# First stage of a decoder trunk: rows of x, norms and rotary tables requested earlier, sums of x halves placed in the weights' order, ordinary units regrouped around products

## The chip, the cores and the metric

The kernel runs on one core of a Trainium2 chip. The metric is device time in microseconds (us) of one execution. Each engine runs its own instructions in the order in which they were issued to it: TensorE (PE in the profile) multiplies, VectorE (DVE) and ScalarE (ACT) work element by element, GpSimd (POOL) does small element-wise work and issues some DMAs, and SyncE (SP) issues most DMAs.

## The reference

A trunk of two layers over x, 256 rows of 2048, in float32. Layer 0 uses differential attention with rotation of the first quarter of each head, layer 1 latent attention; each layer then attends to 256 memory rows and applies a squared-ReLU MLP. Every sub-layer is pre-normed and added to x. The change touches only the beginning of layer 0:

```
h = rms_norm(x, attn_norm[0])
q, k, v = split(h @ da_wqkv, 3)              # 2048 -> 3 x 2048
q = partial_rope(q, cos, sin, 32); k = partial_rope(k, cos, sin, 32)
p = softmax(mask(q k^T / sqrt(128)))         # two maps per head, 8 heads
a = p[map 0] - lam * p[map 1]                # lam from lam_vecs
x = x + rms_norm(a v, subln) * 0.8 @ da_wo
```

The gain of the norm goes into the transposed x ahead of the product; the factor of each row (rstd) is applied behind it, when a product leaves PSUM.

## The kernel before

**A float32 product in three passes.** Each operand is split into a high part in the type that TensorE multiplies fast and a low part, the rest. A product is three matmuls: high x high, high x low, low x high. Activations are split once, weights as they come: a tile of weights (128 x 2048, 1 MB) is loaded by `load` (line 165, SP's queue) into one of seven raw buffers, ACT casts each half of it to `whi` (line 195) and DVE subtracts to get `wlo` (line 196). Four buffers each of `whi` and `wlo` hold two tiles, so ACT and DVE can be two tiles ahead of PE.

**Units and products.** An ordinary unit is one weight tile against both halves of the rows (t = 0, 1): 24 matmuls of 128 x 128 x 512. Where a whole 2048 x 512 projection of both halves of the rows and of two column blocks is wanted, `Seven` and `Chained` compute a 2 x 2 block product with seven products, p1 to p7, instead of eight (in the order p1, p5, p3, p7, p2, p6, p4). A product is two weight tiles of 12 matmuls each, so it uses up weight tiles twice as fast as ordinary units do. Some products take sums of weight blocks: for p5 DVE adds two raw tiles (line 874, `Chained.begin`), for p7, p6 and p4 a POOL DMA adds a block of weights onto a raw tile that an earlier product has used (line 798). The matching sums of x blocks, s1 to s4, are formed once by `GivenForms`: line 459 first adds the high and low part of a given unit of x back together, lines 429, 396 and 397 then form and split the sums.

**Order.** PE's order is written out: the program emits matmuls in sequence, and small tasks (`Task`, a generator that yields delays) are stepped by `pump` when a running count of PE time, `clock`, has passed their due time. So a transpose stands in PE's stream at a place given by its delay, whether or not its input is ready then. The other engines' instructions are ordered by a planner from a simulated timeline, with two exceptions: DMAs keep the program's order on their queue, and instructions marked `in_turn` (the `wlo` subtractions and raw sums) keep the program's order among themselves.

**The first stage.** Four units of x transposed (`xT`) come in with the gains applied (`given_unit`, line 324). Then PE does q of head group 0 (four ordinary units), k of group 0 (four), and three lines, one for each next head group: line gi holds the seven products for q and k of group gi + 1, with eight ordinary units between. In line 0 these are the v of group 0 and the v of group 1; in the other lines, the output projection of the group before and the next v. `diff_line` writes down where the ordinary units stand. Attention of group gi runs as tasks inside line gi.

`take` hands out a split weight tile, refills the list of tiles that are being split, and calls a hook by the number of tiles taken. The hooks bring in what the first units do not need: hook 1 loads the constants (identity, mask, frequencies), hooks 2 to 6 the rows of x in eight pieces of 128 x 512 with a sum of squares by ACT each (line 330), hook 6 also the positions and the vectors for lambda, then rstd (lines 342, 335, 336, 1074), the rotary tables and lambda, and hook 7 starts `GivenForms`.

Behind q and k, `heads_T` evacuates PSUM with the row's factor (line 487, ACT), rotates (lines 498 to 503, six POOL operations), and, after a delay, transposes four heads on PE (line 159) and splits them (lines 296 and 297). With `given` it first waits until the factors have been issued. Its transposes go into the same PSUM bank, or with `spare=True` into a bank from a small side pool.

Of the kernel before, what the change touches and what calls it, by code (L numbers as in the profile page):

```python
# [14 lines left out]
ALU = mybir.AluOpType  # L15
AX = mybir.AxisListType

P = 128
# [11 lines left out]
T_EV, T_TURN, T_ROT, T_SM, T_SQ, T_ADD, T_NORM = 2.6, 2.6, 12.0, 6.5, 4.4, 2.2, 6.5  # L30
# [11 lines left out]
C_ID, C_MASK, C_FREQ, NC_ = 0, 128, 256, 256 + NF  # L42
# [3 lines left out]
def trunk(ctx, tc, x, xT, mem, memT, positions, gcols, gfinal, lam_vecs, consts, W, out):  # L46
    nc = tc.nc
# [19 lines left out]
    def unit():  # L67
        return units.tile([P, 2, 4, S], F32R, tag="unit", name=nm("unit"))
# [78 lines left out]
    def give_back():  # L147
        free_banks[0] += 1
# [12 lines left out]
    def f32(ap):  # L161
        return ap.bitcast(F32)

    def load(dst, src, queue=None):
        tc.keep_in_program_order((queue or nc.sync).dma_start(dst, src))


    def in_turn(ins):
        tc.stamp_issue_order_token(ins.ins, "weights")
        return ins  # L170
# [39 lines left out]
    def fill():  # L210
        while len(ready) < AHEAD and plan:
            job = plan.pop(0)
            if callable(job) and job not in begun:
                job.begin()
            if plan and callable(plan[0]):
                begun.append(plan[0])
                plan[0].begin()
            if callable(job):
                ready.append(job())
            else:  # L220
                name, i, width = job
                ready.append(split_weights(W[name][i, :, : 4 * width], width))

    taken = [0]
    hooks = {}

    def take():
        fill()
        got = ready.pop(0)
        fill()  # L230
        taken[0] += 1
        if taken[0] in hooks:
            hooks[taken[0]]()
        return got

    def unit_part(o, a, h, hi, lo, t, first, last):
# [43 lines left out]
    const = work.tile([P, NC_], F32, tag="ev", name="const", padded_shape=[P, CH], bufs=EVS)  # L280
    g = keep.tile([P, NG], F32, name="g")
    pos = keep.tile([P, NT], I32, name="pos")
    lamv = work.tile([P, 4, P], F32, tag="ev", name="lamv", bufs=EVS)
    xs = [keep.tile([P, D], F32, name=f"x{t}") for t in range(NT)]
    identr = keep.tile([P, P], F32R, name="identr")
    ident = f32(identr)
    maskr = keep.tile([P, P], F32R, name="maskr")
# [88 lines left out]
    class Forms(Stream):  # L376
# [37 lines left out]
        def sums(self):  # L414
            for key in [(t, h) for t in range(NT) for h in range(2)]:
                for task in self.forms[key].tasks:
                    yield task
            for x in range(2):
                views = [self.raw[t][:, 8 * h + 4 * x : 8 * h + 4 * x + 4] for t in range(NT) for h in range(2)]
                for _ in self.sums_of(x, *views):  # L420
                    pass
                yield T_TURN
# [21 lines left out]
    class GivenForms(Forms):  # L444
# [9 lines left out]
        def sums(self):  # L454
            for x in range(2):
                rows = f32(unit()).rearrange("p a k t -> p (a k) t")
                for h in range(2):
                    part = self.units[2 * h + x].tile
                    nc.vector.tensor_tensor(rows[:, 4 * h : 4 * h + 4], f32(part[:, 0]), f32(part[:, 1]), ALU.add)
                    yield T_TURN  # L460
                views = [rows[:, 4 * h : 4 * h + 4, t * P : (t + 1) * P] for t in range(NT) for h in range(2)]
                for _ in self.sums_of(x, *views):
                    yield T_TURN
# [38 lines left out]
        e.tensor_tensor(a, m[0], m[1], ALU.subtract)  # L502
        e.tensor_tensor(b, n[0], n[1], ALU.add)

    def heads_T(ps, t, scale, dst, rot=None, spare=False, given=None):


        def task():
            while given and not given():
                yield 0.5  # L510
            e = evacuate(ps, scale() if given else scale)
            if rot:
                cos, sin, heads, half = rot
                rope(e.rearrange("p (h d) -> p h d", h=heads), cos, sin, heads, half)
            yield T_ROT + (10.0 if given else 0.0) if rot else T_EV
            b = ps
            if spare:
                b = yield from side_bank()
            split(dst, t, transpose4(e, b))
            if spare:  # L520
                give_back()
            yield T_TURN

        dst.run(task())
# [408 lines left out]
    def diff_line(gi):  # L933
        values_of = lambda g: [("da_wqkv", 12 * g + 8 + u, CH) for u in range(4)]
        others = values_of(0) if gi == 0 else [("da_wo", 4 * c + gi - 1, CH) for c in range(4)]
        others = [Item(None, None, [job]) for job in others + values_of(gi + 1)]
        seven = Chained("da_wqkv", 3 * (gi + 1)).items()
        lead = 0 if gi else 3
        line = others[:lead]
        del others[:lead]  # L940
        for n in (1, 1, 1, 1, 1, 2, 1) if gi else (0, 1, 0, 1, 1, 2, 0):
            line += seven[:2] + others[:n]
            del seven[:2], others[:n]
        return line
# [43 lines left out]
    acts = []  # L988
# [21 lines left out]
    def x_pieces(at, n):  # L1010
        for t, c in [(t, c) for t in range(NT) for c in range(4)][at : at + n]:
            xc = xs[t][:, c * CH : (c + 1) * CH]
            load(xc, x[t * P : (t + 1) * P, c * CH : (c + 1) * CH])
            sum_squares(norm.ss[t][:, c : c + 1], xc)

    def first_norm():
        x_pieces(6, 2)
        load(pos, positions)
        load(lamv, lam_vecs)
        norm.rstd = [row_norm(norm.ss[t], D)[:, 0:1] for t in range(NT)]  # L1020
        da_scales.append(keep2(norm.rstd, SC_DA, "rq"))
        da_scales.append(keep2(norm.rstd, 1.0, "r1"))
        tables()

    def tables():

        nc.vector.tensor_copy(posf, pos)
        for t in range(NT):
            nc.vector.tensor_scalar(ang[:, t], const[:, C_FREQ : C_FREQ + NF], posf[:, t : t + 1], None, ALU.mult)
        MAGIC = 1.5 * 2.0**23  # L1030
        PI_LE = 3.1415925
        nc.vector.tensor_scalar(turn, ang, 1.0 / (2.0 * math.pi), MAGIC, ALU.mult, ALU.add)
        nc.vector.tensor_scalar(turn, turn, MAGIC, None, ALU.subtract)
        for part in (6.28125, 0.0019350051879882812, 2.0 * math.pi - 6.28125 - 0.0019350051879882812):
            nc.vector.scalar_tensor_tensor(ang, turn, -part, ang, ALU.mult, ALU.add)
        nc.vector.tensor_scalar(ang, ang, PI_LE, -PI_LE, ALU.min, ALU.max)
        nc.scalar.activation(sin, ang, AF.Sin)
        nc.vector.tensor_scalar(turn, ang, math.pi / 2.0, -2.0 * math.pi, ALU.is_gt, ALU.mult)
        nc.vector.scalar_tensor_tensor(ang, ang, math.pi / 2.0, turn, ALU.add, ALU.add)
        nc.vector.tensor_scalar(ang, ang, PI_LE, -PI_LE, ALU.min, ALU.max)  # L1040
        nc.scalar.activation(cos, ang, AF.Sin)


        lv = lamv.rearrange("p (a b) d -> p a b d", b=2)
        nc.vector.tensor_tensor(lp, lv[:, :, 0, :], lv[:, :, 1, :], ALU.mult)
        nc.vector.tensor_reduce(ls, lp, AX.X, ALU.add)
        nc.scalar.activation(ls, ls, AF.Exp)
        nc.vector.memset(coef, 1.0)
        nc.vector.tensor_tensor(coef[:, 1:2], ls[:, 1:2], ls[:, 0:1], ALU.subtract)
        nc.vector.tensor_scalar(coef[:, 1:2], coef[:, 1:2], -LAMBDA_INIT, None, ALU.add)  # L1050
        nc.vector.tensor_copy(coef[:, 3:4], coef[:, 1:2])
        for i in range(2):
            nc.vector.tensor_scalar(gsub[:, 2 * i : 2 * i + 2], g[:, G_SUB : G_SUB + 2], 1.0 - LAMBDA_INIT, None, ALU.mult)
        nc.scalar.copy(identr, const[:, C_ID : C_ID + P])
        nc.scalar.copy(maskr, const[:, C_MASK : C_MASK + P])
    mem_rstd = []

    def mem_norm():
# [168 lines left out]


    da_scales = []
    hooks[1] = lambda: load(const, consts)  # L1230
    hooks[2] = lambda: x_pieces(0, 1)
    hooks[3] = lambda: x_pieces(1, 1)
    hooks[4] = lambda: x_pieces(2, 2)
    hooks[5] = lambda: x_pieces(4, 2)
    hooks[6] = first_norm
    hooks[7] = lambda: made.append(GivenForms(acts))
    made = []

    hd = DA_ROT // 2

    def rotation(t):
        return cos[:, t, :hd], sin[:, t, :hd], 4, hd
# [53 lines left out]
    for i, dst in enumerate((q, k)):  # L1296
        ps = matmul_chunk(acts)
        for t in range(NT):
            heads_T(ps[t], t, lambda i=i, t=t: da_scales[i][t], dst, rotation(t), given=lambda: da_scales)
    v, before, copied = [], None, {}  # L1300
    free_banks[0] -= 1
    for gi, line in enumerate(diff_lines):
# [32 lines left out]
    acts = norm.done()  # L1335
# [31 lines left out]
    ps = matmul_chunk(acts, LAT)  # L1367
    latent_piece(eq, 0, ps, 0, LAT)
    ps = matmul_chunk(acts, LAT)
# [4 lines left out]
    ps = matmul_chunk(acts, 320)  # L1374
# [186 lines left out]
```

## Time and profile before

| what | value |
|---|---|
| median of 3 runs | 2236.24 us (2235.97 to 2236.39) |
| profiled execution | 2237.54 us |
| its span, first to last instruction | 2235.4 us |
| mean granted TensorE clock | 0.996 |
| HBM read | 499 MB, 224 GB/s over the span |

The profile's page lists busy times by engine and the costliest groups of instructions. The view of windows gives busy times in chosen stretches; the timeline lists instructions in order, and its brackets hold the idle time ahead of an instruction on its engine and what ended it; the chain of waits follows the work that ended last back to the start. In all of them L155 is the matmul helper, L159 the transpose helper, `mm` an ordinary product, `pr` one of the seven, `ax` side work.

### The profile page before, as it was taken

Reading aid. Unit: us, or ns where it says so; the run is one execution under the profiler, and the core shown is the slowest. Engines: PE = TensorE matmul, PEld = TensorE weight load, DVE = VectorE, ACT = ScalarE, POOL = GpSimd, SP = SyncE. Lnnn points to the kernel's source line nnn. Section 1 sums busy time; section 2 is a strip of 40 time slices with the busy share of each in tenths; the row PEclk is TensorE's granted clock in tenths of the full one; section 3 lists DMA queues with packets and bytes.
Section 4 is the critical chain, followed back from the end, with each engine's and each line's share of the span. In section 5 each row is a group of like instructions: output and inputs, shape, how many; then the busy total and the mean of one; then the engine's idle time right before and its main releaser. Section 6 shows DMA issues by size and latency. Waiting matters only on the chain.

```text
span 2235.4 us, 27536 instructions
## 1 busy us (share of the span) xinstructions
PE 2213.1 (99%) x10449; PEld 1842.8 (82%) x10449; DVE 1742.5 (78%) x1921; ACT 1415.4 (63%) x1905; POOL 186.8 (8%) x268
## 2 busy tenths in 40 slices
PE   9999999999999999999999999999999999999998
PEld 7778888888888888888889888888888888888886
DVE  8777877778888888888765766778887887887864
ACT  7666667666666666666645655566666666666664
POOL 0241120000000000000000311000000000000001
PEclk9999999999999999999999999999999999999999
DMA  9679887435886887886945244634688688688691
GB/s 381 177 245 254 268 256 260 162 126 195 270 272 214 264 269 218 263 271 216 294 163 193 87 155 146 256 131 153 231 248 272 234 244 272 235 243 272 228 304 57
DMA packets 75445, 502.96 MB, mean 225 GB/s; under 512 B 8625, under 2 KB 9009, under 8 KB 17201
## 3 DMA queue, kind: packets, MB, share of 16 engines
q1 hardware_dynamic: 64080, 422.56, 50.9%
q0 software_dynamic: 10656, 77.60, 17.8%
q8 instruction: 82, 1.34, 0.2%
q10 hardware_dynamic: 576, 1.05, 0.2%
q14 instruction: 51, 0.41, 0.0%
HBM read 499.08 MB, written 2.10 MB: 224 GB/s over the span
## 4 chain that ended last, share of the span: by engine, by line
PE 91%; DVE 4%; ACT 1%; issue 1%; DMA 1%; POOL 0%; ACTq 0%; POOLq 0%; DVEq 0%
PE mm L155 61%; PE pr L155 24%; PE ax L155 3%; PE ax L159 2%; DVE wlo L196 2%; DVE raw L795 2%; DMA raw<-in_da_wqkv_dram 1%; ACT whi L195 1%; PE mm L159 1%; DVE unit L297 0%; DVE unit L531 0%; DVE raw L874 0%; DVE unit L324 0%; POOL rope L500 0%; DVE unit L711 0%
## 5 line engine op out<-in xcount | busy, mean ns | idle before, releaser
L196 DVE TENSOR_TENSOR wlo<-raw,whi 128x1024 fp32r<-128x1024 f32 (+3 forms) x998 | 1197.2, 1212 | 406.0 <-ACT whi L195 373.8
L195 ACT CAST whi<-raw 128x1024 fp32r<-128x1024 f32 (+3 forms) x998 | 1038.0, 1042 | 687.8 <-PE mm L155 487.2
L155 PE MATMUL mm<-whi,unit 128*128 128x512 f32 (+3 forms) x4160 | 1326.5, 390 | 1.4 <-ACT unit L615 0.9
L155 PEld LDWEIGHTS mm<-whi,unit 128*128 128x128 f32 x4160 | 779.6, 189 | 153.8 <-ACT unit L323 1.3
L155 PE MATMUL mm<-wlo,unit 128*128 128x512 f32 (+3 forms) x2080 | 805.4, 387 | 6.8 <-DVE wlo L196 6.3
L155 PE MATMUL pr<-whi,unit 128*128 128x512 f32 x1904 | 612.9, 391 | 0.0
L155 PEld LDWEIGHTS mm<-wlo,unit 128*128 128x128 f32 x2080 | 392.5, 189 | 86.9 <-DVE wlo L196 15.2
L155 PEld LDWEIGHTS pr<-whi,unit 128*128 128x128 f32 x1904 | 357.4, 188 | 73.8
L155 PE MATMUL pr<-wlo,unit 128*128 128x512 f32 x952 | 370.7, 389 | 0.0
L155 PEld LDWEIGHTS pr<-wlo,unit 128*128 128x128 f32 x952 | 178.9, 188 | 36.3
L798 POOL DMA_DIRECT2D raw<-in_mlp_wup_dram x56 | 49.1, 877 | 1119.0 <-DVE wlo L196 985.2
L795 DVE TENSOR_TENSOR raw<-raw,raw 128x2048 f32<-128x2048 f32 x56 | 127.9, 2284 | 0.0
L482 DVE TENSOR_TENSOR x<-x,mm 128x512 f32<-128x512 f32 x152 | 99.8, 680 | 11.3 <-PE mm L155 10.7
L336 POOL TENSOR_TENSOR rs<-rs,mhalf 128x1 f32<-128x1 f32 (+1 forms) x28 | 26.2, 939 | 556.8 <-DVE rs L335 556.8
L296 ACT CAST unit<-ax 128x512 fp32r<-128x512 f32 (+1 forms) x100 | 55.8, 571 | 25.2 <-PE ax L159 22.7
L297 DVE TENSOR_TENSOR unit<-ax,unit 128x512 fp32r<-128x512 f32 (+1 forms) x100 | 65.4, 663 | 4.4 <-ACT unit L296 1.3
L544 ACT ACTIVATE p<-ax,nmax 128x256 f32<-128x256 f32 (+1 forms) x80 | 33.7, 429 | 29.1 <-DVE nmax L542 28.4
L330 ACT ACTIVATE junk<-x 128x512 bf16<-128x512 f32 x56 | 35.1, 628 | 9.3 <-DVE x L482 8.4
L155 PE MATMUL ax<-unit,unit 128*128 128x256 f32 (+1 forms) x240 | 37.2, 281 | 0.0
L155 PEld LDWEIGHTS ax<-unit,unit 128*128 128x128 f32 x240 | 34.3, 190 | 2.5
L155 PE MATMUL ax<-raw,unit 128*128 128x256 f32 (+1 forms) x240 | 35.3, 279 | 0.8 <-ACT unit L530 0.6
L155 PEld LDWEIGHTS ax<-raw,unit 128*128 128x128 f32 x240 | 32.0, 190 | 2.4 <-ACT unit L530 1.0
(185 smaller groups left out, 1002.3 us busy)
## 6 DMA issues: line engine op xcount, KB each, us to landing
raw<-in_mlp_wup_dram SPq DMA_DIRECT2D x128, 1024.0 KB, 5.2
raw<-in_mlp_wdown_dram SPq DMA_DIRECT2D x128, 1024.0 KB, 5.9
raw<-in_mlp_wup_dram POOLq DMA_DIRECT2D x56, 1024.0 KB, 10.6
raw<-in_da_wqkv_dram SPq DMA_DIRECT2D x45, 1024.0 KB, 9.2
raw<-in_da_wqkv_dram POOLq DMA_DIRECT2D x18, 1024.0 KB, 11.2
raw<-in_da_wo_dram SPq DMA_DIRECT2D x16, 1024.0 KB, 8.4
raw<-in_ca_wkv_dram SPq DMA_DIRECT2D x16, 1024.0 KB, 5.0
raw<-in_mla_wo_dram SPq DMA_DIRECT2D x16, 1024.0 KB, 6.2
```

What stands on the lines that cost most here:

```text
L155: return nc.tensor.matmul(o, stationary, moving, start=start, stop=stop, skip_group_check=not alone)
L159: nc.tensor.transpose(o, src, ident)
L195: nc.scalar.copy(hi, r)
L196: in_turn(nc.vector.tensor_tensor(lo, r, f32(hi), ALU.subtract))
L296: nc.scalar.copy(hi, src)
L297: nc.vector.tensor_tensor(dst[:, 1, :n, t * P : (t + 1) * P], src, f32(hi), ALU.subtract)
L330: nc.scalar.activation(junk[:, : src.shape[1]], src, AF.Square, accum_out=acc)
L336: nc.gpsimd.tensor_tensor(r[:, :n], r[:, :n], mhalf.broadcast_to([P, n]), ALU.pow)
L482: nc.vector.tensor_tensor(xc, xc, ps, ALU.add)
L544: nc.scalar.activation(pr[:, i * w : (i + 1) * w], sb[:, i * w : (i + 1) * w], AF.Exp, bias=nmax[:, i : i + 1], accum_out=ssum[:, i : i + 1],)
L795: in_turn(nc.vector.tensor_tensor(r[p, x], r[p, x], other, ALU.add))
L798: tc.keep_in_program_order(nc.gpsimd.dma_start(o, self.source(*block, x), accum_op=ALU.add))
```

## The change

Four edits, all in the first stage.

- The hooks: constants, positions and x's first two pieces at hook 1; two more pieces, the rotary tables and `GivenForms` at hook 2; two pieces at hook 3; the last two, the vectors for lambda, rstd and lambda at hook 4. The tables and lambda become two functions, with the copies of identity and mask in the first.
- Line 459 is marked `in_turn`.
- The lines of units: for line 0 from O O O p1 p5 O p3 p7 O p2 O p6 O O p4 to O O p1 O p5 O p3 p7 p2 O p6 O O p4 O; for lines 1 and 2 from p1 O p5 O p3 O p7 O p2 O p6 O O p4 O to O p1 O p5 O p3 O p7 p2 O p6 O O p4 O (O is an ordinary unit, each p two tiles).
- `heads_T` for q and k of group 0: a delay of 12 + 12 for q and 12 + 8 for k where both had 12 + 10, and `spare=True`.

```diff
@@ take
         if taken[0] in hooks:
-            hooks[taken[0]]()
+            for hook in hooks[taken[0]]:
+                hook()
@@ GivenForms.sums
-                    nc.vector.tensor_tensor(rows[:, 4 * h : 4 * h + 4], f32(part[:, 0]), f32(part[:, 1]), ALU.add)
+                    in_turn(nc.vector.tensor_tensor(rows[:, 4 * h : 4 * h + 4], f32(part[:, 0]), f32(part[:, 1]), ALU.add))
@@ heads_T
-    def heads_T(ps, t, scale, dst, rot=None, spare=False, given=None):
+    def heads_T(ps, t, scale, dst, rot=None, spare=False, given=None, given_wait=0.0):
...
-            yield T_ROT + (10.0 if given else 0.0) if rot else T_EV
+            yield T_ROT + given_wait if rot else T_EV
@@ diff_line
-        lead = 0 if gi else 3
-        line = others[:lead]
-        del others[:lead]
-        for n in (1, 1, 1, 1, 1, 2, 1) if gi else (0, 1, 0, 1, 1, 2, 0):
+        line, others = (others[:1], others[1:]) if gi else (others[:2], others[2:])
+        for n in (1, 1, 1, 0, 1, 2, 1) if gi else (1, 1, 0, 0, 1, 2, 1):
             line += seven[:2] + others[:n]
@@ first_norm
         x_pieces(6, 2)
-        load(pos, positions)
         load(lamv, lam_vecs)
...
-        tables()
+        lambdas()
@@ tables
         nc.scalar.activation(cos, ang, AF.Sin)
-
+        nc.scalar.copy(identr, const[:, C_ID : C_ID + P])
+        nc.scalar.copy(maskr, const[:, C_MASK : C_MASK + P])
+
+    def lambdas():
...
-        nc.scalar.copy(identr, const[:, C_ID : C_ID + P])
-        nc.scalar.copy(maskr, const[:, C_MASK : C_MASK + P])
@@ hooks
-    hooks[1] = lambda: load(const, consts)
-    hooks[2] = lambda: x_pieces(0, 1)
-    hooks[3] = lambda: x_pieces(1, 1)
-    hooks[4] = lambda: x_pieces(2, 2)
-    hooks[5] = lambda: x_pieces(4, 2)
-    hooks[6] = first_norm
-    hooks[7] = lambda: made.append(GivenForms(acts))
     made = []
+    def tables_in():
+        load(const, consts)
+        load(pos, positions)
+        x_pieces(0, 2)
+
+    def forms_of_x():
+        made.append(GivenForms(acts))
+
+    hooks[1] = (tables_in,)
+    hooks[2] = (lambda: x_pieces(2, 2), tables, forms_of_x,)
+    hooks[3] = (lambda: x_pieces(4, 2),)
+    hooks[4] = (first_norm,)
@@ q and k of group 0
-            heads_T(ps[t], t, lambda i=i, t=t: da_scales[i][t], dst, rotation(t), given=lambda: da_scales)
+            heads_T(ps[t], t, lambda i=i, t=t: da_scales[i][t], dst, rotation(t), given=lambda: da_scales, given_wait=8.0 if i else 12.0, spare=True)
```

## The prediction

> **What bounds the kernel now.** I read the page first (busy shares and costliest groups), then the windows of 20 us, then the timeline and the chain at the places where a window holds too few matmuls.
>
> ```profile
> span 2235.4 us, 27536 instructions
> PE 2213.1 (99%) x10449; PEld 1842.8 (82%) x10449; DVE 1742.5 (78%) x1921; ACT 1415.4 (63%) x1905; POOL 186.8 (8%) x268
> L196 DVE TENSOR_TENSOR wlo<-raw,whi 128x1024 fp32r<-128x1024 f32 (+3 forms) x998 | 1197.2, 1212 | 406.0 <-ACT whi L195 373.8
> 60.00:80.00 20.00, 17.08 (x66) 13.59 (x66) 10.50 (x9) 7.49 (x8) 8.80 (x23) 0.83 0.29 73
> 140.00:160.00 20.00, 17.15 (x84) 13.93 (x83) 16.66 (x21) 14.80 (x22) 8.27 (x14) 0.98 0.57 213
> 160.00:180.00 20.00, 20.00 (x78) 16.23 (x79) 16.56 (x16) 8.79 (x10) 7.56 (x4) 0.85 0.86 233
> ```
>
> TensorE is busy 99% of the span, so only its 22 us of idle time and its slow stretches can be won. The three windows (columns: PE, PEld, DVE, ACT, POOL busy with counts, granted clock, DMA share, GB/s) show where: PE is idle 2.9 us in the first and 2.9 us in the second, and in the first and third the granted clock is 0.83 and 0.85. The timeline and the chain size the three places:
>
> ```profile
> 60.51 0.39 PE L155 MATMUL mm<-whi,unit 128*128 128x512 f32 x1
> 61.65 0.66 PE L159 MATMUL mm<-identr,ev 128*128 128x128 f32 x4 [0.75 <-POOL ev L503]
> 64.47 1.12 PE L159 MATMUL mm<-identr,ev 128*128 128x128 f32 x4 [2.16 <-POOL ev L503]
> 65.58 10.51 PE mm L155 x36
> 76.09 5.45 PE pr L155 x24
> 81.54 0.87 PE mm L159 x8
> 156.54 0.39 PE L155 MATMUL mm<-whi,unit 128*128 128x512 f32 x1
> 159.78 8.37 PE mm L155 x23
> 168.15 5.44 PE pr L155 x24
> 253.64 0.39 PE L155 MATMUL mm<-whi,unit 128*128 128x512 f32 x1
> 254.82 5.51 PE mm L155 x23
> 260.33 0.44 PE ax L159 x4
> ```
>
> At full clock a matmul costs 5.44/24 = 0.227 us and eight transposes 0.87.
> Place A, the transposes of the rotated q: from 60.51 + 0.23 = 60.74 to 76.09 lie 15.35 us for eight transposes and 36 matmuls, 0.87 + 8.16 = 9.03. Lost: **6.3 us**.
> Place B, the first ordinary unit behind the seam of groups 0 and 1 (products p4, p1): from 156.54 to 168.15, 11.61 us for 24 matmuls of 5.44. Lost: **6.2 us**.
> Place C, the same seam of groups 1 and 2: from 253.64 to 260.33, 6.69 us for 5.44. Lost: **1.2 us**.
> At A and B about half is idle time, the rest the halved clock behind it (23 matmuls in 8.37 us is 0.36 each).
>
> **The change, part by part.** *Rows of x, norms, tables.* What is late at A:
>
> ```profile
> 30.60 3.20 SPq L165 DMA_DIRECT2D x<-in_x_dram  x2
> 34.11 0.33 SPq L165 DMA_DIRECT2D pos<-in_positions_dram  x1
> DMA to landing us min/median/max: 9.0/11.2/12.7
> 48.05 0.16 DVE L1027 CAST posf<-pos 128x2 f32<-128x2 int32 x1
> 53.73 0.68 ACT L487 ACTIVATE ev<-mm,rq 128x512 f32<-128x512 f32 x1
> 59.23 0.27 ACT L1041 ACTIVATE cos<-ang 128x96 f32<-128x96 f32 x1
> 59.58 1.18 POOL L498 TENSOR_TENSOR rope<-ev,cos 128x64 f32<-128x64 f32 x1 [0.68 <-ACT cos L1041]
> 61.00 0.32 POOL L502 TENSOR_TENSOR ev<-rope,rope 128x64 f32<-128x64 f32 x1
> 20.00:40.00 20.00, 20.00 (x25) 1.00 1.02 409
> ```
>
> The positions are asked for at 34.11, behind all of x; the angles begin at 48.05, cos ends at 59.50, and only then the rotations run. The change asks for them behind the constants, at the first unit and not the sixth (five units of 5.4 us sooner), and forms the tables at the second: this link goes. Next is the norm. The last piece of x, issued at 33.5 and landing 9.0 to 12.7 us later, stood behind ten weight tiles and will stand behind eight; DMA is full there (409 GB/s, DVE window row, share 1.02), so it lands 2 x 1.05 MB / 409 = 5.1 us sooner. With the same lag behind it, the evacuation of q's second half (53.73 + 0.68 = 54.4) ends about 49.3.
> What is wanted sooner too: the planner's delay was 22 counted from the sixth unit and is 24 from the end of q's chunk; counted in matmuls the transposes stand 24 (5.4 us) further forward, at 60.74 - 5.44 = 55.3 us. From 49.3 there are 6.0 us for one rotation of six POOL operations.
>
> ```profile
> 137.00:144.00 7.00, 7.00 (x34) 5.81 (x33) 4.32 (x6) 3.41 (x5) 5.80 (x12) 1.00 1.01 328
> ```
>
> Two rotations took 5.80 us of POOL beside a working DVE, so 2.9 for one: ready at 52.2, 3.1 us ahead. A's whole 6.3 us goes. Bounds: 6.3 if that holds, about 0 if the rotations wait (rival 2); I take 6.0. k's transposes, due some 18 us later, lie behind no late link. spare=True puts these transposes in a side bank and frees q's and k's banks at their evacuation: no instruction more.
> The row of POOL at 59.58 took 1.18 us where that at 61.00 took 0.32. [...]
>
> What is moved past what on SP's queue: constants, positions and x's first pieces go ahead of the next weight tile, and at most four pieces of 0.26 MB more than now stand ahead of any tile, 1.05 MB or 2.6 us. The cover is in ACT:
>
> ```profile
> 18.92 0.33 SPq L165 DMA_DIRECT2D raw<-in_da_wqkv_dram  x1
> 41.90 1.06 ACT L195 CAST whi<-raw 128x1024 fp32r<-128x1024 f32 x1 [0.21 <-PE mm L155]
> 18.56 2.35 DVE L459 TENSOR_TENSOR unit<-unit 128x1024 f32<-128x1024 f32 x2
> 24.69 0.61 PE L155 MATMUL mm<-whi,unit 128*128 128x512 f32 x2
> 25.43 0.50 PE L155 MATMUL mm<-wlo,unit 128*128 128x512 f32 x1
> ```
>
> The tile asked for at 18.92 is cast some 20 us later, and the cast then waits for PE to release a buffer, not for data: the moved DMAs cost nothing. If squares of x stood in ACT's line ahead of casts before their rows land, that cover is gone (rival 3).
>
> *The order of sums of x halves.* At 18.56 two of these additions ran ahead of the low parts of a unit that PE soon wanted; PE then waited from 24.69 + 0.45 to 25.43, 0.3 us. Held in the order of the weights, they come later; nothing wants them before p5, at about 74 us. Worth 0 to 0.3 us; I take 0.2. The table and norm operations are the same ones, earlier.
>
> *Ordinary units at the seam.* A product's half wants 1.2 us of DVE for 1.36 us of PE, an ordinary half the same 1.2 for 2.72. So a run of four product tiles (p4, p1) with transposed outputs between lives from the two tiles held in advance:
>
> ```profile
> 155.12 2.28 DVE L874 TENSOR_TENSOR raw<-raw,raw 128x2048 f32<-128x2048 f32 x1
> 157.32 1.28 DVE L297 TENSOR_TENSOR unit<-ax,unit 128x512 fp32r<-128x512 f32 x2
> 158.52 2.34 DVE L196 TENSOR_TENSOR wlo<-raw,whi 128x1024 fp32r<-128x1024 f32 x2
> ```
>
> At B the low part wanted at 156.9 stood behind 2.28 + 1.28 us of other work. With two ordinary units at the seam DVE gets 2 x (5.44 - 2.42) = 6.0 us there, twice the 2.85 that was missing: B and C go, 7.4 us. The price is paid inside the groups: p7 and p2 now touch in every group, and in group 0 p3, p7, p2 run on for six tiles. In group 0 before, p3 and p7 ran with an ordinary unit behind:
>
> ```profile
> 94.80:107.90 13.10, 13.10 (x68) 11.06 (x67) 10.96 (x21) 12.36 (x26) 1.75 (x2) 1.00 0.49 151
> 107.90:113.60 5.70, 5.70 (x29) 4.68 (x28) 5.70 (x9) 2.44 (x5) 0.00 (x0) 1.00 1.05 213
> 94.80:107.90 13.10, 7.19 (x6) 1.00 0.49 151
> 107.90:113.60 5.70, 4.77 (x4) 1.00 1.05 213
> ```
>
> The last two rows are the low parts (line 196) alone. In 18.8 us DVE made 10 of them beside 16.66 - 11.96 = 4.7 us of attention and value work. Four product tiles (10.9 us) filled 13.1 us of PE there, so 2.2 went to attention; six with the same 2.2 fill 18.5, in which 10 low parts are wanted, since two tiles lie ready ahead. DVE's total of 16.66 fits with 1.8 us to spare, and ACT's 12.36 + 2.44 = 14.80 too; their waits for each other may eat that. No wait is added beside these; ACT, DVE and PE keep their counts. Bounds for new waits: 0, and 6.2 at one place (B's price). I take 0.5 us here, nearer to the row that fits, and 0.5 for the rest of the kernel, whose order the planner may shift.
>
> Sum: 6.0 + 0.2 + 7.4 - 1.0 = 12.6 us. The profiled execution took 2237.54 us (its span 2235.4 and 2.1 around it): 2224.9. The median of the runs shown, 2236.24, lies 1.3 lower: **2223.6 us**.
>
> **The rivals.**
> 1. The long run in group 0 falls dry once, gap and slow clock as at B: 12.6 - 6.2 = 6.4 gained, 2229.8 us. For it: DVE is busy 5.70 of 5.70 us behind p7. Against it: the sum above fits. [...]
> 2. The q transposes are late as before, since x still lands late or DVE shuts out the rotations: A's 6.0 stays, 2229.6 us. For it: the rotations' operations at 0.48 us where one alone takes 0.32; against it: 3.1 us in hand.
> 3. The change does not do what it says for the first chunk: ACT's line takes squares of x before their rows land (9.0 us at least behind the issue) and casts wait. At 25 us nothing is held in advance (PE waits at 25.43), so a wait of 5 us counts whole, and the slow clock behind it as at B, 6.2 - 2.9 = 3.3: 8.3 us, 2231.9. Against it: before, no square waited for its row.
> 4. Slower: p7 and p2 back to back fall dry in each of the three groups, a seam moved and not removed: 3 x 6.2 = 18.6 lost for 12.6 gained, 2242.2 us. It decides from the point where three dry runs cost over 4.2 us each. Against it: groups 1 and 2 have an ordinary unit ahead of p7.
>
> **How the numbers follow.** Chances: forecast 0.64; rival 1 0.12; rival 2 0.10; rival 3 or more than one rival together 0.08; rival 4 0.06. The forecast's own range is 2221.5 to 2227; drawn to rivals 1 and 2 it is 2221.5 to 2231, and what is left out is rivals 3 and 4. A measurement here tells 0.2% from no change, 4.5 us: faster is below 2231.8. Faster 0.64 + 0.12 + 0.10 = 0.86, same 0.08, slower 0.06.
>
> **What would show it.** Right: no idle PE ahead of the transposes at 55 us, granted clock 1.00 in all windows from 20 to 300 us, 24 ordinary matmuls in 5.4 to 5.5 us at both seams. Wrong: PE waiting for line 196 in p2 or the unit behind it; PE waiting for line 503; ACT idle for rows of x before 30 us; a halved clock anywhere new.

## The result, and the profile after

| | before | after |
|---|---|---|
| median | 2236.43 us (2235.97 to 2239.85, 6 runs) | 2227.60 us (2226.17 to 2228.65, 6 runs) |
| ratio | | 0.9957 (95% interval 0.9945 to 0.9970) |
| profiled execution | 2237.54 us | 2228.04 us, span 2226.3 |

The change gains 8.8 us where the prediction summed 12.6. The helper lines of the changed kernel carry numbers one higher than before (L298 was L297, L460 was L459, L504 was L503), and the transposes of q now bear the name `ax`.

The page of the changed kernel, and its windows of 20 us (columns as before: PE, PEld, DVE, ACT, POOL busy, clock, DMA share, GB/s):

```profile
span 2226.3 us, 27536 instructions
PE 2208.0 (99%) x10449; PEld 1840.5 (83%) x10449; DVE 1744.5 (78%) x1921; ACT 1416.8 (64%) x1905; POOL 185.4 (8%) x268
```

```profile
20.00:40.00 20.00, 20.00 (x90) 16.57 (x89) 16.11 (x30) 15.12 (x28) 0.00 (x0) 1.00 1.03 406
40.00:60.00 20.00, 18.73 (x88) 15.40 (x87) 19.55 (x31) 15.52 (x26) 15.51 (x15) 1.00 0.92 360
60.00:80.00 20.00, 19.88 (x92) 16.16 (x91) 18.14 (x18) 11.94 (x15) 9.69 (x14) 1.00 0.36 88
150.00:170.00 20.00, 20.00 (x98) 16.82 (x97) 18.54 (x18) 12.28 (x14) 1.79 (x2) 1.00 0.46 114
```

No instruction came or went: 27536 in all, and the counts of PE, DVE, ACT and POOL are those of before. PE is busy 5.1 us less (2213.1 before), the halved clock's share (mean granted clock 0.996 before, 0.998 after), and the rest of the gain is idle time. From 20 us on the clock is 1.00 in these windows, and the seam that held place B is full.

The chain that ended last, at the two later seams, after:

```profile
154.59 5.45 PE pr L155 x24
160.04 0.44 PE ax L159 x4
160.48 5.45 PE mm L155 x24
...
245.64 5.44 PE pr L155 x24
251.08 0.44 PE ax L159 x4
251.52 5.49 PE mm L155 x24
```

The ordinary units behind p1 need 5.45 and 5.49 us for 24 matmuls, where they took 11.61 and 6.69: B and C are gone.

What is still lost shows in PE's timeline, as brackets with the idle time and its cause:

```profile
10.13 0.79 PE L155 MATMUL mm<-whi,unit 128*128 128x512 f32 x1 [2.27 <-ACT unit L324]
11.15 1.05 PE L155 MATMUL mm<-whi,unit 128*128 128x512 f32 x2
...
43.98 0.39 PE L155 MATMUL mm<-wlo,unit 128*128 128x512 f32 x1
...
57.36 0.60 PE L159 MATMUL ax<-identr,ev 128*128 128x128 f32 x4
59.23 0.66 PE L159 MATMUL ax<-identr,ev 128*128 128x128 f32 x4 [1.27 <-POOL ev L504]
```

The first is new: a wait of 2.27 us in the first weight tile, with the clock halved behind it (0.50 in the window from 9.97 to 13.37 us; two matmuls in 1.05 us). In the profile of before, the same low-part matmul as that at 43.98 stands here:

```profile
41.92 0.39 PE L155 MATMUL mm<-wlo,unit 128*128 128x512 f32 x1
```

So the changed kernel's execution ran 2.06 us late by then. The wait comes before the first instruction that the change moves, the load of the positions (SP's timeline; it stood at 34.11):

```profile
15.82 0.33 SPq L165 DMA_DIRECT2D pos<-in_positions_dram  x1
```

The transposes at 59.23 are what is left of A: the second four of q wait 1.27 us for the last of the six rotation operations. The ACT instruction that ends the first wait stands behind ACT's cast of the third piece of the first weight tile, and that cast waited for its load:

```profile
9.05 0.62 ACT L195 CAST whi<-raw 128x512 fp32r<-128x512 f32 x1 [2.46 <-DMA raw<-in_da_wqkv_dram]
```

### The profile page after: what moved, and what is told of

Its sections match the earlier page's. It is cut to its first block, busy times and chain, and to the rows that moved or that the text cites. A ratio compares the mean times of both kernels' runs of the same rounds, so it can differ in the third digit from the quotient of the medians.

```text
span 2226.3 us, 27536 instructions
## 1 busy us (share of the span) xinstructions
PE 2208.0 (99%) x10449; PEld 1840.5 (83%) x10449; DVE 1744.5 (78%) x1921; ACT 1416.8 (64%) x1905; POOL 185.4 (8%) x268
## 3 DMA queue, kind: packets, MB, share of 16 engines
q10 hardware_dynamic: 576, 1.05, 0.2%
## 4 chain that ended last, share of the span: by engine, by line
PE 93%; DVE 4%; ACT 1%; issue 1%; POOL 0%; DMA 0%; ACTq 0%; POOLq 0%; DVEq 0%
PE mm L155 62%; PE pr L155 25%; PE ax L155 3%; PE ax L159 2%; DVE raw L796 2%; DVE wlo L196 2%; ACT whi L195 1%; PE mm L159 1%; DMA raw<-in_da_wqkv_dram 0%; DVE unit L298 0%; DVE unit L460 0%; DVE unit L398 0%; POOL rs L337 0%; POOL rope L499 0%; DVE raw L875 0%
## 5 line engine op out<-in xcount | busy, mean ns | idle before, releaser
L196 DVE TENSOR_TENSOR wlo<-raw,whi 128x1024 fp32r<-128x1024 f32 (+3 forms) x998 | 1197.3, 1212 | 399.6 <-ACT whi L195 367.2
L297 ACT CAST unit<-ax 128x512 fp32r<-128x512 f32 (+1 forms) x104 | 57.8, 571 | 26.2 <-PE ax L159 23.7
L298 DVE TENSOR_TENSOR unit<-ax,unit 128x512 fp32r<-128x512 f32 (+1 forms) x104 | 68.0, 665 | 4.4 <-ACT unit L297 1.3
```

Of the source, the lines that this page charges most:

```text
L196: in_turn(nc.vector.tensor_tensor(lo, r, f32(hi), ALU.subtract))
L297: nc.scalar.copy(hi, src)
L298: nc.vector.tensor_tensor(dst[:, 1, :n, t * P : (t + 1) * P], src, f32(hi), ALU.subtract)
```

## The experiments

The theory at the outset: the seam edit and the row edit each remove one place; what is missing against 12.6 us is A's remainder, the start, and the fact that the terms of A and B held a share of halved clock which not every execution pays. The rivals: the wait at the start belongs to the change; new waits inside the groups eat the gain; an edit valued at nothing costs or earns something.

### Both kernels a second time

No edit: the changed kernel five times more, the kernel before once.

> The changed kernel unaltered, a second time. In its first profile 2.05 us were lost between 7.4 and 14 us, where ACT waited for the first weight tile (rows of DMA, landing at 9.05) and the clock then fell; ACT's and DVE's lines are the same there as before. My theory: a late DMA of that execution, not of the change; then this profile's 25th matmul-pass on low parts of the fourth tile starts near 25.4 us as before and the profiled time is near 2226. Rival: it belongs to the changed kernel; then the wait near 9 us is there again and the time is near 2228. In both, q's second transposes wait 1.3 to 1.5 us near 57 us, and the ordinary unit behind p1 starts 0.5 us late three times.

> The kernel before, profiled a second time. My theory (the wait near 9 us comes by chance): no sure answer from one look, but the wait can show here too, and then the profiled time is near 2239.5. Rival (only the changed kernel has it): never here, 2237 to 2238. The three places A, B and C are there in both, with 6.3, 6.2 and 1.2 us.

Measured: the changed kernel 2226.15 us (2225.88 to 2227.74), ratio 0.9958 (0.9945 to 0.9972); the kernel before once, 2235.09 us, shorter than either theory had it and without the wait at 9 us. In the changed kernel both waits are there again in other sizes, the one at the start as the rival had it, though the time is the theory's. PE's timeline:

```profile
9.79 0.50 PE L155 MATMUL mm<-whi,unit 128*128 128x512 f32 x1 [1.89 <-ACT unit L324]
57.13 0.65 PE L159 MATMUL ax<-identr,ev 128*128 128x128 f32 x4 [0.67 <-POOL ev L504]
```

In the kernel before, place B again, in PE's timeline and in the chain (the 23 matmuls behind the gap):

```profile
158.29 0.50 PE L155 MATMUL mm<-wlo,unit 128*128 128x512 f32 x1 [2.87 <-DVE wlo L196]
```

```profile
158.29 7.12 PE mm L155 x23
```

The gap is the 2.85 us of the first profile, but the 23 matmuls behind it take 7.12 us and not 8.37: the granted clock was 0.50 for 3.4 us (the window from 159.0 to 162.4), not for 6.8 (159.1 to 165.9 in the first profile). At A the same execution has its two gaps and no halved clock: PE is busy 7.08 of the 10 us from 60 to 70 in both profiles, at 1.00 here and at 0.68 in the first. Matmul by matmul it gains 2.8 us at A and about 1.2 at B on the first profile, loses some 1.4 in small waits elsewhere, and ends 2.45 us shorter than the execution from which the prediction was made.

### Each half of the change alone

Only the new lines of units, on the kernel before:

```diff
-        lead = 0 if gi else 3
-        line = others[:lead]
-        del others[:lead]
-        for n in (1, 1, 1, 1, 1, 2, 1) if gi else (0, 1, 0, 1, 1, 2, 0):
+        line, others = (others[:1], others[1:]) if gi else (others[:2], others[2:])
+        for n in (1, 1, 1, 0, 1, 2, 1) if gi else (1, 1, 0, 0, 1, 2, 1):
```

> The kernel before with the new order of ordinary units alone. My theory: places B and C go, 7.4 us, and 0.5 us come back at each of three ordinary units behind p1, as seen after the change; place A stays with 6.3. So 5.9 us gained, ratio 0.9974, about 2230.5. Rival (the runs p3 p7 p2 fall dry without the earlier tables): PE waits in group 0 again, about 2235.

All the rest of the change, with the old lines of units (the diff above, taken back):

> The changed kernel with the old order of units, so rows of x, norms, tables, delays, side banks and the order of sums alone. My theory: place A shrinks from 6.3 to 1.5 us, 4.8 gained and up to 0.3 more at the start; B and C stay with 7.4. So about 2231.4, ratio 0.9978. Rival (the two parts are not independent, the seam was late because of A): B and C shrink too, about 2227.

Measured: units alone 2230.42 us (2228.01 to 2233.77, 11 runs), ratio 0.9978 (0.9970 to 0.9987); the rest alone 2233.86 us (2230.86 to 2235.43, 11 runs), ratio 0.9988 (0.9979 to 0.9997). The medians lie 5.4 and 1.9 us under before's 2235.78: the seam edit carries most of the gain, as expected, and the row edit, on which the prediction had put 6.0 us, gains 1.9; its median lies 2.5 us above what I expected and far above the rival's 2227. The two parts add up to 7.3 us where the whole gained 9.6 beside the same runs of before; the intervals, 2 to 3 us to either side, are too wide to call that an interaction. In the second kernel B stays, and shows once more how much of it is chance (PE's timeline, and the chain behind the gap):

```profile
157.66 0.50 PE L155 MATMUL mm<-wlo,unit 128*128 128x512 f32 x1 [2.65 <-DVE wlo L196]
```

```profile
157.66 5.51 PE mm L155 x23
```

A gap of 2.65 us, and then 23 matmuls in 5.51 us, with the clock at 1.00 from 158 to 168: no lost clock at all. Three profiles of one place give 8.37, 7.12 and 5.51 us for the same work behind nearly the same gap.

### Mending what is left

First, the transposes of q 3 us later; second, an ordinary tile split ahead of the next product's raw addition, so that the 2.28 us addition no longer stands in front of the low part that PE wants; third, both.

```diff
@@ q and k of group 0 (first and third)
-  given_wait=8.0 if i else 12.0, spare=True)
+  given_wait=8.0 if i else 15.0, spare=True)
@@ take's refill (second and third)
+            late = not callable(job) and job[0] in ("da_wqkv", "da_wo")
+            if late:
+                name, i, width = job
+                ready.append(split_weights(W[name][i, :, : 4 * width], width))
...
+            if late:
+                continue
```

> The changed kernel with the delay of q's transposes raised from 12 + 12 to 12 + 15, so that they stand two parts (12 matmuls, 2.7 us) later in PE's line. My theory: the rotation of q's second half ends at 59 us, some 1.5 us behind its place; moved by 2.7 us the wait goes: 1.3 to 1.5 us gained on the changed kernel's 2226.2 to 2227.6. Rival (the rotation slides with PE, as its norm waits for work that PE paces): the wait stays near 1.4 us and the time is the same. In both the wait for the first weight tile near 8 us may or may not show; if it comes by chance, some start shows none.

> The changed kernel with the raw addition for the next product placed behind the split of an ordinary unit's tile instead of ahead of it. My theory: at the ordinary unit behind p1 the low part waits for the 2.28 us addition that the order of the weights puts ahead of it; placed behind, the three late starts of 0.5 us go and nothing else: 1.5 us gained. Rival (DVE is short there whatever the order): the same 0.5 us come back at p5, same time.

> The two edits of q later and addition behind together. My theory: they are independent, 2.8 to 3.0 us gained on the changed kernel, so about 2224. Rival: one takes the other's gain, about 2225.5.

Measured, beside before's 2235.28 us: 2225.44 (2224.63 to 2227.37), 2225.78 (2225.66 to 2227.22) and 2224.11 us (2223.63 to 2224.95). In the first, PE has no wait at q's transposes any more. For the second I had taken the late starts of the units behind p1 too large: counted from matmul to matmul, the profile of the changed kernel shows only one that can be measured, 0.51 us where 0.23 is due, at 73.4 us. Neither edit alone stands clear of the changed kernel. With both, all five times lie below all eleven of the changed kernel; but the kernel before, too, ran 0.5 and 1.2 us shorter here than beside those two series, and the intervals of the ratios overlap (0.9935 to 0.9960 here, 0.9945 to 0.9972 for the changed kernel), so a further gain is likely and not shown. The two windows around A in the profile of both together:

```profile
20.00:40.00 20.00, 20.00 (x90) 16.56 (x89) 16.74 (x31) 16.29 (x30) 2.07 (x1) 1.00 1.03 406
40.00:60.00 20.00, 20.00 (x94) 16.64 (x93) 20.00 (x32) 15.68 (x25) 15.09 (x18) 1.00 0.94 383
```

PE is full in both. In this profile, and in that of the second edit alone, there is no wait of 2 us at 9 us either, though the loads of the first 10 us stand in the same order. In the 14 profiles of this study the cast of the third piece begins after 7.9 us in eight: twice with the changed kernel and once each with the units alone, the rest alone, the first edit here, and three of the experiments below. Four of these eight load x as the kernel before does, and four kernels that load it as the changed one does are free of the late cast. So the wait at the start comes and goes with either order of loads: as far as 14 profiles tell, it is chance and not the change's work.

### The order of the sums

The changed kernel with line 460 set free; then the kernel before with that one mark added; then the free order with q's transposes 6 us later.

```diff
@@ first: the changed kernel
-                    in_turn(nc.vector.tensor_tensor(rows[...], f32(part[:, 0]), f32(part[:, 1]), ALU.add))
+                    nc.vector.tensor_tensor(rows[...], f32(part[:, 0]), f32(part[:, 1]), ALU.add)
@@ third: the first, and
-  given_wait=8.0 if i else 12.0, spare=True)
+  given_wait=8.0 if i else 18.0, spare=True)
```

> The changed kernel with the sums of x halves not held in the weights' order (that part undone). My theory: DVE then forms half of them between 18 and 35 us, where it was idle 3.9 of 20 us after the change, and is freer at 44 to 59 us, where POOL's six operations of q's second rotation took 6.35 us beside a DVE busy 19.55 of 20; that rotation takes under 5 us, the wait near 57 us shrinks by 1 us or more, and up to 0.3 us come back as a late low part near 25 us: 0.7 to 1.2 us gained. Rival (the norm is late by itself): rotation and wait as they are, same time or 0.3 us slower.

> The kernel before with only the sums of x halves (line 459) put into the weights' order; PE's stream is the same. Theory 1 (the order has a worth only together with the sooner rows: alone, the positions are still asked for at 34.1 us, so the rotary tables stay late and the q transposes with them): 0 to 1 us faster, 2234.5 to 2236. Theory 2 (the order frees DVE between 20 and 40 us by itself, and what was lost when it was undone in the changed kernel, about 4 us, is found here too): 2231 to 2232.5.

> The changed kernel with the sums of x halves free of the weights' order, as in e8_sums_free, and the delay of q's transposes 12 + 18 where it had 12 + 12, so that they stand 6 us later. Theory 1 (all that the free order cost lies in q's transposes waiting for late rotary tables, 1.41 + 2.10 us of gap and the halved clock behind it): those gaps vanish and the time is 2225.5 to 2227. Theory 2 (the free order also costs elsewhere): 2228.5 to 2230.5.

Measured. Free order in the changed kernel: 2230.26 us (2229.26 to 2232.50, 9 runs), ratio 0.9976 (0.9967 to 0.9986), 2.7 to 4.1 us slower than the changed kernel's two medians, where a gain was expected. Order alone in the kernel before: 2245.50 us (2242.68 to 2249.69, 5 runs), ratio 1.0045 (1.0033 to 1.0058), 9.3 us slower than before and outside both theories. Free order with later transposes: 2224.73 us (2224.33 to 2227.84, 5 runs), ratio 0.9955 (0.9942 to 0.9969), a little better than the first theory had it.

Where the four additions of halves ran is one row of the view by source line in each kernel: the kernel before, the changed one, the changed one with free order, the kernel before with the order alone.

```profile
L459 DVE TENSOR_TENSOR unit<-unit x4: 1217/1218/1219, 18.6 to 35.7; 128x1024 f32<-128x1024 f32 x4
```

```profile
L460 DVE TENSOR_TENSOR unit<-unit x4: 1211/1218/1339, 35.7 to 53.1; 128x1024 f32<-128x1024 f32 x4
```

```profile
L460 DVE TENSOR_TENSOR unit<-unit x4: 1218/1218/1219, 18.6 to 34.5; 128x1024 f32<-128x1024 f32 x4
```

```profile
L459 DVE TENSOR_TENSOR unit<-unit x4: 1210/1278/1344, 61.0 to 81.5; 128x1024 f32<-128x1024 f32 x4
```

Free, they and the sums that follow fill DVE from 20 us on, and the small table operations stand between them. In the changed kernel cos is done at 35.35 us; with the free order it is not, and PE waits at A. The changed kernel's ACT timeline, then window, ACT and PE timeline of the free order:

```profile
35.08 0.27 ACT L1039 ACTIVATE cos<-ang 128x96 f32<-128x96 f32 x1
```

```profile
20.00:40.00 20.00, 20.00 (x90) 16.58 (x89) 20.00 (x31) 14.84 (x27) 0.00 (x0) 1.00 1.03 406
```

```profile
55.31 0.28 ACT L1039 ACTIVATE cos<-ang 128x96 f32<-128x96 f32 x1
```

```profile
57.16 0.66 PE L159 MATMUL ax<-identr,ev 128*128 128x128 f32 x4 [1.41 <-POOL ev L504]
59.92 0.77 PE L159 MATMUL ax<-identr,ev 128*128 128x128 f32 x4 [2.10 <-POOL ev L504]
```

DVE is busy 20.00 of 20 us, as in the kernel before, against 16.11; the tables are 20.2 us later, and with them the rotations. Setting q's transposes 6 us later removes those two waits and the whole of the cost: 2224.73 us is level with the 2225.44 of the sums held in order and q's transposes 3 us later. So the cost lay there.

In the kernel before, the order alone sends the additions past the wish of p5, the first product in line 0 that uses a raw sum (PE's timeline):

```profile
80.53 0.79 PE L155 MATMUL pr<-wlo,unit 128*128 128x512 f32 x1 [3.17 <-DVE wlo L196]
89.32 0.80 PE L155 MATMUL pr<-whi,unit 128*128 128x512 f32 x1 [4.55 <-ACT unit L396]
92.14 1.22 PE L155 MATMUL pr<-whi,unit 128*128 128x512 f32 x2 [1.60 <-DVE unit L397]
```

That is 9.3 us of gaps, and the halved clock behind them (0.66 in the mean from 80 to 100 us). There `GivenForms` starts at the seventh tile, so the turn of the additions falls behind seven tiles' low parts; in the changed kernel it starts at the second. q's transposes, on the other hand, did not wait in that run: DVE was busy 11.75 of the 20 us from 20 to 40, and POOL's rotation, released by cos, went on at 56.06, 3.5 us sooner than before (59.58), though the positions were asked for no sooner in the program. Place A thus went, 6.1 us from matmul to matmul, with no row of x moved. Still the mark in line 460 has no worth by itself: it trades DVE's time for the tables against DVE's time for the sums, and in these runs it paid only with `GivenForms` at the second tile.

### The place of the transposes alone

The kernel before with the new lines of units, `heads_T`'s edit, and only the delays changed: rows, norms, tables, `GivenForms` and the order of sums stay where they were. Two versions:

```diff
-  rotation(t), given=lambda: da_scales)
+  rotation(t), given=lambda: da_scales, given_wait=10.0 if i else 16.0, spare=True)   # first
+  rotation(t), given=lambda: da_scales, given_wait=13.0 if i else 16.0, spare=True)   # second
```

> The kernel before with the new lines of units and with heads_T's edit alone, the delay of q's transposes 12 + 16 where the kernel before has 12 + 10: neither rows, norms, tables nor the order of sums are moved. The first transposes stand 6 us later and want the rotated q at about 69 us; it was ready at 64 to 66 us. Theory 1 (place A is only a place in PE's stream, so a number moves it out of the wait as well as all the sooner rows do): no PE wait at the q transposes, 2225.5 to 2227.5, as fast as the changed kernel. Theory 2 (the sooner rows are needed; the wait moves along, or turns up at the k transposes or at the sums for p5): 2229 to 2231, as with the new lines of units alone.

> As e11_delay_alone (the new lines of units, heads_T's edit, rows and tables and sums where they were before), with the delay of k's transposes 12 + 13 where that run and the kernel before have 12 + 10, so that they stand 3 us later. Theory 1 (what that run lacks to the changed kernel is the 1.2 us at k's transposes, at 79 us, which the two rotations behind a working DVE miss): no wait there, 2226 to 2227.5, level with the changed kernel. Theory 2 (rows, norms and tables in time are needed for more than these transposes): still 2228 or above.

Measured: 2228.25 us (2226.31 to 2229.31), ratio 0.9965 (0.9952 to 0.9977), between the two theories; with k's transposes later too, 2226.99 us (2225.62 to 2228.29), ratio 0.9953 (0.9940 to 0.9967), as the first theory had it. In the first version q's eight transposes run in one go and k's second four wait (PE's timeline), since k's rotation runs beside DVE's additions (timelines of POOL and DVE):

```profile
68.11 1.03 PE L159 MATMUL ax<-identr,ev 128*128 128x128 f32 x8
...
78.97 0.66 PE L159 MATMUL ax<-identr,ev 128*128 128x128 f32 x4 [1.20 <-POOL ev L503]
```

```profile
66.53 0.32 POOL L499 TENSOR_TENSOR rope<-ev,sin 128x64 f32<-128x64 f32 x1
66.81 1.32 POOL L500 TENSOR_TENSOR rope<-ev,cos 128x64 f32<-128x64 f32 x1
68.09 2.37 POOL L501 TENSOR_TENSOR rope<-ev,sin 128x64 f32<-128x64 f32 x1
```

```profile
66.72 1.23 DVE L196 TENSOR_TENSOR wlo<-raw,whi 128x1024 fp32r<-128x1024 f32 x1 [1.31 <-ACT whi L195]
67.86 2.41 DVE L874 TENSOR_TENSOR raw<-raw,raw 128x2048 f32<-128x2048 f32 x1
```

Two delays and the lines of units are thus level with the whole change (2226.15 and 2227.60 in its two comparisons), and their ratio, 0.9953, with the 0.9954 and 0.9955 of the versions above that move the rows and set q's transposes later (0.9948 with the second edit as well). Within these intervals, moving the rows, norms and tables forward brought nothing that a later place for eight transposes each of q and k does not bring.

## Why the prediction was right and where it was not

**The seams (7.4 us): right in mechanism, too large in size.** Both seams run at full rate. Between the first two profiles, counted from matmul to matmul, they gave 7.2 us; in medians the units alone gain 5.4. Of B's 6.2 us, 2.85 is the gap, which came in all three profiles; the rest came behind it, with the clock at 0.50 for 6.8, 3.4 and 0 us, as 3.2, 1.9 and 0.3 us (8.37, 7.12 and 5.51 less 23 x 0.227 = 5.22). The prediction counted the dearest of the three as the price.

**Rows, norms and tables (6.0 us): the step that failed.** It read "With the same lag behind it, the evacuation of q's second half (53.73 + 0.68 = 54.4) ends about 49.3", and then "Two rotations took 5.80 us of POOL beside a working DVE, so 2.9 for one: ready at 52.2, 3.1 us ahead". Between the first two profiles, counted from matmul to matmul, A gave 4.6 us; the whole edit alone gave 1.9 in medians. After the change (timelines of DVE, POOL and ACT), and the last square of x in ACT's timeline before:

```profile
45.81 0.14 DVE L343 TENSOR_REDUCE tot<-ss 128x1 f32<-128x4 f32 x1
48.01 0.14 DVE L336 TENSOR_SCALAR rs<-tot 128x1 f32<-128x1 f32 x1
51.81 0.14 DVE L1073 TENSOR_SCALAR rq<-rs 128x1 f32<-128x1 f32 x1
```

```profile
44.08 0.79 POOL L499 TENSOR_TENSOR rope<-ev,cos 128x64 f32<-128x64 f32 x1 [1.98 <-ACT ev L488]
...
48.96 1.53 POOL L337 TENSOR_TENSOR rs<-rs,mhalf 128x1 f32<-128x1 f32 x1
52.82 1.64 POOL L499 TENSOR_TENSOR rope<-ev,cos 128x64 f32<-128x64 f32 x1 [2.33 <-ACT ev L488]
54.42 1.31 POOL L500 TENSOR_TENSOR rope<-ev,sin 128x64 f32<-128x64 f32 x1
...
58.41 0.76 POOL L504 TENSOR_TENSOR ev<-rope,rope 128x64 f32<-128x64 f32 x1
```

```profile
43.90 0.62 ACT L331 ACTIVATE junk<-x 128x512 bf16<-128x512 f32 x1
51.98 0.69 ACT L488 ACTIVATE ev<-mm,rq 128x512 f32<-128x512 f32 x1 [1.28 <-DVE rq L1073]
```

```profile
48.29 0.63 ACT L330 ACTIVATE junk<-x 128x512 bf16<-128x512 f32 x1
```

The last square of x begins 4.4 us sooner than before (43.90 against 48.29), near the 5.1 that were predicted. But the evacuation ends at 52.67 and not at 49.3, since the lag did not stay the same: from the start of that square to the end of the evacuation it is 8.8 us, where it was 6.1. DVE's three small steps (the rows above) now stand among larger operations of a full DVE and come some 2 us later behind their inputs; the power for the second half's rstd (48.96) stands on POOL behind the first rotation, which before ran after it, and that adds 0.7. Then the second rotation takes 52.82 to 59.17, 6.35 us, not 2.9. The row that gave 2.9 had DVE busy 4.32 of 7.00 us; here it is busy 19.55 of 20. The place, on the other hand, was reckoned rightly: q's transposes begin at 57.36, 55.3 without the late start, and so the change itself had asked for q 5.4 us sooner.

The six operations of that second rotation took 0.65 to 1.64 us each. In the rows around 68 us above one took 0.32 us begun with DVE idle, 1.32 beside a 1.23 us low part, 2.37 beside a 2.41 us addition. Six operations as long as a low part (1212 ns in the mean of line 196) would make 7.3 us, an estimate nearer to the 6.35 than the row's 2.9. How the wait of 1.27 us came out is in part luck, since the rotation began later than reckoned and the late start moved the transposes back too.

**What set the size of A.** The prediction treated A as lateness of data. The two delays show that it was as much a place in PE's stream: a number for each of q and k moves the place at no cost that was measured, while the sooner rows ran into a busy DVE. And the lateness itself was not only the late request for the positions: with the order of sums alone, the request as late as before, A's wait was gone.

**The order of sums (0 to 0.3 us, 0.2 taken): wrong.** The bound looked only at PE's wait at 25 us and at the wish of p5. In the changed kernel, with q's transposes where they stand, the order is worth 2.7 to 4.1 us, since it empties DVE for the tables; alone it costs 9.3. "Nothing wants them before p5" is true, but the prediction did not work out when their turn would come.

**The moved DMAs (nothing) and the new waits (1.0 us): right.** PE is full from 20 to 40 us. In the long run p3 p7 p2 each low part is ready 1.4 us or more ahead of its matmul; one new late start, 0.28 us, shows behind p1. (The working counted ten low parts for those six tiles; with two tiles ready ahead they need eight of their twelve, so it erred on the safe side.)

**The sum.** The profiled executions differ by 2237.54 - 2228.04 = 9.5 us against 12.6, 3.1 short. The start has 2.06 of it, which is chance, and A's remainder, 1.27 where 0.3 was left, has 1.0: together 3.0. The median of 2227.60 lies 0.6 above the forecast's own range and within the range that takes in rivals 1 and 2; the second series, 2226.15, lies within the forecast's own. The step from 2224.9 to 2223.6 was a mistake of its own. The profiled execution of before lay 1.3 us above the median because it paid more halved clock at A and B (granted clock 0.996; of before's other executions those at 0.996 took 2236.18 us or more, those at 0.998 at most 2235.40), and that is just what the change takes away; the offset could not be taken off a second time. 2224.9 would have been the forecast by the same terms; the three versions of the changed kernel whose profiles show no wait at A have medians of 2224.11, 2224.73 and 2225.44.

**The rivals.** The long run did not fall dry, ACT did not wait for rows of x, and p7 p2 did not move the seam into the groups. Rival 2, late transposes, happened in part, through a rotation of 6.35 us beside a busy DVE: 1.27 us of it (its 0.48 us for an operation is 5.80 over the 12 of the row from 137 to 144). Of the signs named, PE's wait for the rotation was seen, and the halved clock in a new place too, but at the start and by chance.

## What to carry to other kernels

When PE waits for a side result, ask first whether its place in PE's stream can be moved back; making the result sooner moves more instructions and may, as here, run into the engine that is full. Expect small steps on that engine to come later too (here some 2 us). Take the duration of a GpSimd operation from a row with the same DVE load as the place it will stand in: a rotation was put at 2.9 us from a row with DVE busy 4.32 of 7.00 us, and took 6.35 where DVE was busy 19.55 of 20. A gap's halved clock was a lottery here (0.3, 1.9 and 3.2 us lost behind nearly the same gap): price a gap at its own length for sure and the clock as a range, and never correct for an execution that was long because of the very loss you remove.

## What the runs showed of the hardware

The same gap on PE cost different clock. Behind gaps of 2.85, 2.87 and 2.65 us at one place the granted clock was 0.50 for 6.8, 3.4 and 0 us; in the kernel before with the order alone PE was idle 2.97 of the 20 us from 160 to 180, and the clock was 1.00. The 3.4 us from 159.00 to 162.40 read, in the second profile of before and in the kernel with the old lines of units and all the rest of the change:

```profile
159.00:162.40 3.40, 3.40 (x10) 2.62 (x9) 3.40 (x3) 0.00 (x0) 3.40 (x1) 0.50 0.60 173
```

```profile
159.00:162.40 3.40, 3.40 (x17) 2.82 (x16) 3.40 (x3) 1.05 (x1) 3.40 (x1) 1.00 0.82 253
```

PE counts 10 matmuls in the one and 17 in the other. In the first profile of before the clock was at 0.50 from 63.5 to 70.4 us, at A, and from 159.1 to 165.9, at B, 6.8 us each; in that of the changed kernel from 10.0 to 13.4, 3.4 us, at a gap of 2.27. In the run with the order alone, the mean of 0.66 over the 20 us from 80 to 100 makes 13.6 us at 0.50. What decides whether the clock falls at a gap, and for how long, was not shown.

The first megabyte also lands unevenly: the cast of the third of the first tile's four pieces begins at 6.83 to 9.05 us in the 14 profiles, under the same order of loads, and each of the eight late ones shows as a wait of 1.2 to 2.3 us on PE (2.27 in the changed kernel's first profile, 1.89 in its second). What delays the load was not tried.
